# A macaron decoder layer in split float32 on one core: gate and up products of 16 of 22 inner blocks by seven products of sums of blocks

## The chip, the cores and the metric

One NeuronCore of a Trainium2 chip runs the whole layer in one launch. The metric is the device time of the program in microseconds (us); lower is better. The kernel before was run three times.

## The reference

One decoder layer over 512 tokens of width 1024: a SwiGLU half-step, a mixer (retention and causal block attention on one combined projection, then an output projection), and a second SwiGLU half-step. What the change touches are the two half-steps:

```
def _swiglu(h, w_gate, w_up, w_down):
    return (jax.nn.silu(h @ w_gate) * (h @ w_up)) @ w_down
...
    x = x + 0.5 * _swiglu(_rms(x, ffn1_norm_w[l]), ffn1_w_gate[l], ffn1_w_up[l], ffn1_w_down[l])
...
    x = x + 0.5 * _swiglu(_rms(x, ffn2_norm_w[l]), ffn2_w_gate[l], ffn2_w_up[l], ffn2_w_down[l])
```

`w_gate` and `w_up` are 1024 x 2816 and `w_down` is 2816 x 1024, all float32. Each half-step normalises `x` by its root mean square over the features first.

## The kernel before

Features lie on the partitions and the 512 tokens along the free axis, so every weight chunk is a 128x128 stationary operand and the moving operand is 128x512. Every float32 operand is split into two float32r parts, H by a copy on ScalarE and L = x - H by a subtraction on VectorE; one product is then three matmuls, WH.xH + WH.xL + WL.xH (`mm3`).

`ffn` (called twice) goes over FB = 22 inner blocks of 128 features. For each it loads the 128x1024 chunks of gate and up weights, splits them (`split_w`, tiles `raw`, `wh`, `wl`, three buffers each) and issues 2 x 8 x 3 = 48 matmuls of 512 columns into two PSUM banks (`p` for gate, `s` for up). VectorE then multiplies both by the reciprocal root mean square `st.r`, ScalarE applies Silu, VectorE multiplies the two and the result is split for the down product. The down product goes over KB = 8 output blocks with 22 x 3 = 66 matmuls each and adds half of the result to the residual; `nxt` hands each finished block to the next stage. `Stream.add` squares each residual block on ScalarE and adds the squares up, on GpSimd (`nc.gpsimd.tensor_add`); `Stream.stats` makes `st.r` of them. The mixer lies between the two half-steps.

The order of instructions is not that of the code. `Plan` notes every call, then `_order` runs a list schedule over a table of costs (`_cost`, `LAT`) with the slot counts of each tile tag as limits, and issues every engine's queue in that order. `DELAYS` shifts the parts of the mixer in it. All recorded calls have one line in the profile (L181).

## Time and profile before

| | us |
|---|---|
| three runs | 1012.77, 1010.34, 1012.0 |
| median | 1012.0 |
| the profiled execution: its span, first to last instruction | 1010.4 |
| PE busy | 993.1 |
| VectorE (DVE) busy | 526.2 |
| ScalarE (ACT) busy | 413.3 |
| GpSimd (POOL) busy | 88.8 |

The profiled execution has no time of its own beside its span; the span is 1.6 us below the median of the runs. PE is busy for 98% of it. Matmuls are pipelined, so the duration of one (0.39 us for 512 columns) is longer than the step from one to the next; the step is what counts. On VectorE too an instruction may start before the duration of the one ahead of it has run out.

### The profile page before, as it was taken

The numbers are of one execution on the slowest core, as the hardware profiler recorded it, in microseconds if no ns is written. First come the engines' busy times: TensorE is split into PE (matmuls) and PEld (weight loads), VectorE is DVE, ScalarE is ACT, GpSimd is POOL, SyncE is SP. The second block draws the span as 40 slices with busy tenths as digits, with TensorE's granted clock in tenths as the row PEclk, the third lists the DMA queues.
The fourth block names the chain that finished last, engine by engine and source line by source line (L and its number), as shares of the span: only waits on it lengthen the run. The fifth ranks groups of instructions, "written<-read, shape, count | busy, mean of one in ns | idle before, by whom it ended". The sixth has DMA issues, their size and how long they took to land.

```text
span 1010.4 us, 11674 instructions
## 1 busy us (share of the span) xinstructions
PE 993.1 (98%) x4524; PEld 812.5 (80%) x4524; DVE 526.2 (52%) x768; ACT 413.3 (41%) x641; POOL 88.8 (9%) x63
## 2 busy tenths in 40 slices
PE   8999999999999999989999999999999999999998
PEld 4888888888888888878887778688888888888888
DVE  7535434534332325587879997855445445432231
ACT  6423223223222225467868876543233233221120
POOL 4000000000010100143213320400000000000000
PEclk9999999999999999999999999999999999999999
DMA  6322322332333463352233211422322322333330
GB/s 222 117 92 84 114 95 84 106 103 78 111 116 105 131 211 115 107 151 66 83 131 115 58 38 53 141 103 86 105 94 94 104 91 97 99 94 110 125 111 26
DMA packets 36407, 105.17 MB, mean 104 GB/s; under 512 B 4480, under 2 KB 6528, under 8 KB 36352
## 3 DMA queue, kind: packets, MB, share of 16 engines
q1 hardware_dynamic: 36352, 104.43, 32.1%
q8 instruction: 35, 0.57, 0.2%
q14 instruction: 20, 0.16, 0.0%
HBM read 97.60 MB, written 4.19 MB: 101 GB/s over the span
## 4 chain that ended last, share of the span: by engine, by line
PE 87%; DVE 7%; ACT 3%; issue 1%; DMA 1%; SPq 0%; DVEq 0%; ACTq 0%
PE ps_p L181 45%; PE ps_s L181 36%; DVE s L181 5%; PE ps_t L181 4%; ACT s L181 2%; PE ps_o L181 2%; DVE wl L181 1%; ACT wh L181 1%; DMA s<-in_x_t_dram 1%; SPq L181 0%; DVE c L181 0%; DVE ad L181 0%; ACT c L181 0%; DVEq L181 0%; ACT cr L181 0%
## 5 line engine op out<-in xcount | busy, mean ns | idle before, releaser
L181 PE MATMUL ps_p<-s,wh 128*128 128x512 f32 (+1 forms) x1548 | 561.8, 392 | 3.1 <-DVE s L181 1.6
L181 PE MATMUL ps_s<-s,wh 128*128 128x512 f32 (+1 forms) x1056 | 399.1, 385 | 0.0
L181 ACT ACTIVATE wh<-raw 128x1024 fp32r<-128x1024 f32 (+4 forms) x186 | 181.0, 976 | 469.7 <-PE ps_p L181 335.7
L181 PEld LDWEIGHTS ps_p<-s,wh 128*128 128x128 f32 x1548 | 289.6, 189 | 67.0 <-DVE s L181 3.4
L181 PE MATMUL ps_p<-s,wl 128*128 128x512 f32 (+1 forms) x774 | 298.3, 392 | 1.7 <-DVE wl L181 1.7
L181 DVE TENSOR_TENSOR wl<-raw,wh 128x1024 fp32r<-128x1024 f32 (+4 forms) x186 | 219.3, 1182 | 131.4 <-ACT wh L181 128.7
L181 PEld LDWEIGHTS ps_s<-s,wh 128*128 128x128 f32 x1056 | 198.6, 188 | 39.5 <-ACT wh L181 0.2
L181 PE MATMUL ps_s<-s,wl 128*128 128x512 f32 (+1 forms) x528 | 203.6, 386 | 1.5 <-DVE wl L181 1.5
L181 PEld LDWEIGHTS ps_p<-s,wl 128*128 128x128 f32 x774 | 145.7, 189 | 32.2 <-DVE wl L181 2.9
L181 ACT ACTIVATE s<-s 128x512 f32<-128x512 f32 (+2 forms) x216 | 134.1, 628 | 77.5 <-DVE s L181 66.8
L181 DVE TENSOR_TENSOR s<-ps_p,s 128x512 f32<-128x512 f32 x72 | 49.5, 688 | 190.8 <-PE ps_p L181 190.0
L181 POOL TENSOR_TENSOR s<-s 128x512 f32<-128x512 f32 x57 | 87.5, 1542 | 376.5 <-ACT s L181 290.6
L181 DVE TENSOR_TENSOR s<-s 128x512 fp32r<-128x512 f32 (+2 forms) x155 | 111.8, 723 | 15.7 <-ACT s L181 8.6
L181 PEld LDWEIGHTS ps_s<-s,wl 128*128 128x128 f32 x528 | 99.1, 188 | 22.7 <-DVE wl L181 3.2
L181 DVE TENSOR_TENSOR s<-ps_s,s 128x512 f32<-128x512 f32 x44 | 30.4, 691 | 52.5 <-PE ps_s L181 50.2
L181 PE MATMUL ps_o<-s 128*128 128x256 f32 (+3 forms) x144 | 39.7, 295 | 2.3 <-DVE s L181 2.1
L181 PE MATMUL ps_t<-wh,s 128*128 128x512 f32 x96 | 33.7, 395 | 0.0
L181 PEld LDWEIGHTS ps_o<-s 128*128 128x128 f32 x144 | 27.3, 189 | 6.8 <-ACT s L181 2.5
L181 DVE SCALAR_TENSOR_TENSOR s<-s 128x512 f32<-128x512 f32 x30 | 24.1, 807 | 11.8 <-ACT s L181 11.5
L181 DVE SCALAR_TENSOR_TENSOR s<-s,cols 128x512 fp32r<-128x512 f32 (+1 forms) x28 | 26.8, 967 | 5.8 <-ACT s L181 5.8
L181 DVE SCALAR_TENSOR_TENSOR s<-ps_p,s 128x512 f32<-128x512 f32 (+1 forms) x9 | 6.0, 662 | 31.1 <-PE ps_p L181 31.1
L181 PE MATMUL ps_s<-s 128*128 128x128 f32 (+3 forms) x64 | 19.0, 336 | 2.8 <-DVE s L181 2.8
(65 smaller groups left out, 387.3 us busy)
## 6 DMA issues: line engine op xcount, KB each, us to landing
raw<-in_wg_dram SPq DMA_DIRECT2D x43, 512.0 KB
raw<-in_wu_dram SPq DMA_DIRECT2D x43, 512.0 KB
raw<-in_wd_dram SPq DMA_DIRECT2D x32, 512.0 KB
raw<-in_w_int_dram SPq DMA_DIRECT2D x20, 512.0 KB
raw<-in_wd_dram SPq DMA_DIRECT2D x16, 384.0 KB
s<-in_rtab_dram SPq DMA_DIRECT2D x16, 256.0 KB
raw<-in_w_inn_dram SPq DMA_DIRECT2D x8, 512.0 KB
raw<-in_w_o_dram SPq DMA_DIRECT2D x8, 384.0 KB
```

What stands on the lines that cost most here:

```text
L181: self.ops.append([eng, cost, lambda: fn(*args, **kwargs), deps, tiles, i + self.delay + DELAYS.get(self.part, 0), self.part])
```

## The change

Of the 22 inner blocks the first EVEN = 6 stay as they were. The other 16 are taken in 8 pairs (block q with block q + 8). For a pair, the weights of each of gate and up form a 2 x 2 arrangement of parts (block one or two; first or last four of the eight 128-feature chunks), and the normalised activations form a 2 x 2 arrangement too (chunk q with chunk q + 4; first or last 256 tokens). Seven products of sums of such parts (`strassen`, the Winograd form) take the place of eight. Each product is 2 (gate, up) x 4 chunks x 3 = 24 matmuls with 256 columns, both in one PSUM bank; gate in the left half, up in the right. `weave` notes the products of a pair between those of the next.

The activations' seven blocks are made once in each half-step (`token_blocks`); since they hold the normalised `x`, the products of the 16 blocks need no multiplication by `st.r`. The residual blocks give up their slots, so `x` is loaded again from DRAM before the down product (from `x_t`, or from `later`, which the mixer's output is now stored to). All added sums, of weights, activations and products, are on VectorE, and so are the sums of squares that were on GpSimd.

Weights are loaded and split in pieces of 128x512 in place of 128x1024 (768 and 256 for `w_down`), out of one pool of 98 slots of 128x512 that also holds everything else (before: 80 such slots and nine 128x1024 tiles). All eight PSUM banks have one tag with a limit for each use. The planner's table changes: a matmul costs 13.3 ns over its columns in place of 3, a GpSimd instruction somewhat more, and two-input SBUF instructions of VectorE and GpSimd are taken to exclude one another. `DELAYS` is as it was.

```diff
+EVEN = 6
+HALF = (22 - EVEN) // 2
...
-            return max(480.0, out.nbytes() / 380.0)
+            chip = all("DRAM" not in str(a.space) for a in [out, *ins])
+            return max(650.0 if chip else 480.0, out.nbytes() / 390.0)
...
-            return max(107.0, n * 0.4167) + 3
+            return max(107.0, n * 0.4167 + 13.3)
...
-        return 45 + n * 2.31
+        return 45 + n * 2.45
...
+        shared = eng == "POOL" or eng == "DVE" and sum(
+            self._free(a) > 1 and "PSUM" not in str(a.space) for a in ins) > 1
...
+                        if ops[pick][7]:
+                            other = "POOL" if e == "DVE" else "DVE"
+                            busy[e] += max(0.0, share[other] - t)
+                            share[e] = busy[e]
...
-    NS, NRAW, NSPLIT = 80, 3, 3
+    NS = 98
...
+    SLOTS = {"raw": 12, "sum": 4, "wh": 6, "wl": 6, "keep": 4, "row": 8, "block": 32}
+    BANKS = {"p": 2, "s": 2, "t": 3, "o": 1, "a": 2, "b": 2, "c": 2}
...
+        each = 512 // shape[2]
+        raws, hs, ls = [], [], []
+        for a in range(0, shape[1], each):
+            n = min(each, shape[1] - a)
+            tiles = slot(use="raw"), slot(F32R, use="wh"), slot(F32R, use="wl")
+            raw, h, lo = (t[:, :n * shape[2]].rearrange("p (a b) -> p a b", a=n) for t in tiles)
+            for x, to in zip((raw, h, lo), (raws, hs, ls)):
+                to.append(x)
+            if pieces is None:
+                nc.sync.dma_start(raw, src[:, a:a + n])
+                nc.scalar.activation(h, raw, AF.Copy)
...
-                nc.gpsimd.tensor_add(self.ssq, self.ssq, sq)
+                nc.vector.tensor_add(self.ssq, self.ssq, sq)
...
+    def token_blocks(pairs, gates=None):
+        res = [[] for _ in range(7)]
+        gate = lambda q: setattr(nc, "after", gates and gates[min(q, len(gates) - 1)])
+        for q, (one, two) in enumerate(pairs):
+            gate(q)
+            if q % 2 == 0:
+                bh, bl = slot(F32R, use="block"), slot(F32R, use="block")
+            o = slice(256 * (q % 2), 256 * (q % 2) + 256)
+            nc.scalar.activation(bh[:, o], one[:, :256], AF.Copy)
+            nc.vector.tensor_sub(bl[:, o], one[:, :256], f32(bh[:, o]))
+            res[0].append((bh[:, o], bl[:, o]))
+        def two_blocks(n, t):
+            h, lo = split(t, use="block")
+            for i in range(2):
+                res[n + i].append((h[:, 256 * i:256 * i + 256], lo[:, 256 * i:256 * i + 256]))
+        for q, (one, two) in enumerate(pairs):
+            gate(q)
+            two_blocks(1, two)
+        later = []
+        for q, (one, two) in enumerate(pairs):
+            gate(q)
+            t = slot(use="block")
+            nc.vector.tensor_sub(t[:, :256], one[:, 256:], one[:, :256])
+            nc.vector.tensor_sub(t[:, 256:], two[:, 256:], t[:, :256])
+            two_blocks(3, t)
+            u = slot(use="block")
+            nc.vector.tensor_sub(u[:, :256], two[:, 256:], one[:, 256:])
+            nc.vector.tensor_sub(u[:, 256:], two[:, :256], t[:, 256:])
+            later.append(u)
+        for q, u in enumerate(later):
+            gate(q)
+            two_blocks(5, u)
+        nc.after = None
+        return res
+    def strassen(load, nk, moving, taken):
+        n = nk * 128
+        r = {}
+        for i, j in ((1, 1), (1, 2), (2, 1), (2, 2)):
+            r[i, j] = [slot(use="raw")[:, :n] for _ in range(2)]
+            for m in range(2):
+                load(r[i, j][m], m, i, j)
+        s1 = [slot(use="sum")[:, :n] for _ in range(2)]
+        s = [s1, s1, r[2, 1], r[1, 2]]
+        for m in range(2):
+            nc.vector.tensor_add(s1[m], r[2, 1][m], r[2, 2][m])
+        for m in range(2):
+            nc.vector.tensor_sub(s[2][m], r[1, 1][m], r[2, 1][m])
+        banks, marks = {}, []
+        def product(tag, w, block, said):
+            start = tag not in banks
+            if start:
+                banks[tag] = bank(tag)
+            p = banks[tag]
+            marks.append(len(nc.ops) + 2)
+            for m in range(2):
+                h, lo = slot(F32R, use="wh")[:, :n], slot(F32R, use="wl")[:, :n]
+                nc.scalar.activation(h, w[m], AF.Copy)
+                nc.vector.tensor_sub(lo, w[m], f32(h))
+                out = p[:, 256 * m:256 * m + 256]
+                for k in range(nk):
+                    o = slice(k * 128, k * 128 + 128)
+                    xh, xl = moving[block][k]
+                    for a, (ww, xx) in enumerate(((h, xh), (h, xl), (lo, xh))):
+                        nc.tensor.matmul(out, ww[:, o], xx, start=start and m + k + a == 0,
+                                         stop=k == nk - 1 and a == 2, skip_group_check=True)
+            taken(said, p)
+        yield marks
+        product("a", r[1, 1], 0, "P1")
+        yield marks
+        product("c", r[1, 2], 1, "P2")
+        yield marks
+        product("b", s[0], 3, "P5")
+        for m in range(2):
+            nc.vector.tensor_sub(s1[m], s1[m], r[1, 1][m])
+        product("a", s[1], 4, "U2")
+        for m in range(2):
+            nc.vector.tensor_sub(s[3][m], r[1, 2][m], s1[m])
+        yield marks
+        product("a", s[2], 5, "U3")
+        yield marks
+        product("a", r[2, 2], 6, "C21")
+        product("b", s[3], 2, "B")
+        yield marks
+    def weave(calls):
+        run, marks = None, None
+        for call in [*calls, None]:
+            nxt = call and call(marks)
+            if nxt:
+                new = next(nxt)
+            for n in range(2):
+                if run:
+                    next(run)
+                if nxt:
+                    next(nxt)
+            if run:
+                next(run)
+            if nxt:
+                marks = new
+            run = nxt
+        return marks
+    def ffn(st, x, wg, wu, wd, nxt, was, first=None, last=False):
+        hs = [None] * FB
+        for fb in range(EVEN):
...
+        pairs = []
+        for q in range(4):
+            two = []
+            for kb in (q, q + 4):
+                t = slot(use="block")
+                nc.vector.scalar_tensor_tensor(t, x[kb], st.nw[:, kb:kb + 1], st.r,
+                                               op0=OP.mult, op1=OP.mult)
+                two.append(t)
+            pairs.append(two)
+        blocks = token_blocks(pairs)
+        def hidden(one, two):
+            def load(t, m, i, j):
+                nc.sync.dma_start(t.rearrange("p (a b) -> p a b", a=4),
+                                  (wg, wu)[m][(one, two)[i - 1]][:, 4 * j - 4:4 * j])
+            rows = [[slot(use="row") for _ in range(2)] for _ in range(2)]
+            keep = {}
+            def add(i, j, p, old):
+                for m in range(2):
+                    o = slice(256 * m, 256 * m + 256)
+                    nc.vector.tensor_add(rows[i][m][:, 256 * j:256 * j + 256], p[:, o], old[:, o])
+            def taken(what, p):
+                if what in ("P1", "U2", "U3"):
+                    keep[what] = slot(use="keep")
+                    nc.scalar.activation(keep[what], p, AF.Copy)
+                elif what == "P5":
+                    keep[what] = p
+                if what == "P2":
+                    add(0, 0, p, keep["P1"])
+                elif what == "U3":
+                    add(1, 1, keep["P5"], keep["U3"])
+                    g, u = (t[:, 256:] for t in rows[1])
+                    nc.scalar.activation(g, g, AF.Silu)
+                    hs[two] = slot()
+                    nc.vector.tensor_mul(hs[two][:, 256:], g, u)
+                elif what == "C21":
+                    g = rows[1][0][:, :256]
+                    nc.scalar.activation(g, p[:, :256], AF.Silu)
+                    nc.vector.tensor_mul(hs[two][:, :256], p[:, 256:], g)
+                elif what == "B":
+                    add(0, 1, p, keep["U2"])
+                    g, u = rows[0]
+                    nc.scalar.activation(g, g, AF.Silu)
+                    hs[one] = slot()
+                    nc.vector.tensor_mul(hs[one], g, u)
+            return strassen(load, 4, blocks, taken)
+        marks = weave([lambda _, q=q: hidden(q, q + HALF) for q in range(EVEN, EVEN + HALF)])
+        nc.after = marks[-1]
         for db in range(KB):
-            # the last block of all by halves of the tokens, so that less is left after the products
+            x[db] = slot()
+            nc.sync.dma_start(x[db], was[db])
+        nc.after = None
+        order = [*range(FB - 1 - HALF), *range(FB - HALF, FB - 1), FB - 1 - HALF, FB - 1]
+        parts = {}
+        for fb in order:
...
+        nc.sync.dma_start(later[db], x[db])
```

On PE, in the first half-step. Before, the gate and up products of a block alternate, all with 512 columns (`ps_p` gate, `ps_s` up, `s` the activations):

```order
L181 MATMUL ps_p<-s,wh 128x512
L181 MATMUL ps_s<-s,wl 128x512
L181 MATMUL ps_p<-s,wh 128x512
L181 MATMUL ps_s<-s,wh 128x512
L181 MATMUL ps_p<-s,wl 128x512
L181 MATMUL ps_s<-s,wh 128x512
```

Now (weights are in `s` too, banks are `ps`):

```order
L196 MATMUL ps<-s 128x512 x67
L196 MATMUL ps<-s,cr 128x512
L196 MATMUL ps<-s 128x512 x2
L196 MATMUL ps<-s,cr 128x512
L196 MATMUL ps<-s 128x512 x219
L196 MATMUL ps<-s 128x256 x1296
L196 MATMUL ps<-s 128x512 x7
L196 MATMUL ps<-s 128x256 x48
L196 MATMUL ps<-s 128x512 x563
```

After the 288 matmuls of six blocks and four of the statistics stand 1344 of 256 columns in place of 768 of 512, with the first seven of the down product ahead of the last 48; the same row of 1296, 7 and 48 stands in the second half-step.

On VectorE, in the middle of the gate and up stage. Before, one inner block (`ps_p`, `ps_s`: products taken out of PSUM; `wl`: the low part of a weight chunk):

```order
L181 TENSOR_TENSOR s<-ps_p,s 128x512
L181 TENSOR_TENSOR wl<-raw,wh 128x1024
L181 TENSOR_TENSOR s<-ps_s,s 128x512
L181 TENSOR_TENSOR s<-s 128x512
L181 TENSOR_TENSOR wl<-raw,wh 128x1024
L181 TENSOR_TENSOR s<-s 128x512
```

Now, one pair of inner blocks (the third of eight):

```order
L196 TENSOR_TENSOR s<-ps,s 128x256 x2
L196 TENSOR_TENSOR s<-s 128x512
L196 TENSOR_TENSOR s<-s 128x256
L196 TENSOR_TENSOR s<-ps,s 128x256 x2
L196 TENSOR_TENSOR s<-s 128x512 x5
L196 TENSOR_TENSOR s<-ps,s 128x256
L196 TENSOR_TENSOR s<-s 128x512 x3
L196 TENSOR_TENSOR s<-ps,s 128x256 x2
L196 TENSOR_TENSOR s<-s 128x512 x14
```

A pair has 23 instructions of 512 columns (14 low parts of weights, 8 sums of weights, one product of gate and up) and 8 of 256; in the fifth, sixth and seventh pair the last run is 20 long, with six low parts of finished inner blocks in it.

On VectorE at the start of the program. Before (`s<-s,cols`: low parts of the weighted input; `TENSOR_SCALAR s<-ps_t`: the statistics):

```order
L181 SCALAR_TENSOR_TENSOR s<-s,cols 128x512 x3
L181 TENSOR_TENSOR wl<-raw,wh 128x1024 x3
L181 TENSOR_TENSOR s<-s 128x512
L181 TENSOR_SCALAR s<-ps_t 128x512
```

Now:

```order
L196 SCALAR_TENSOR_TENSOR s<-s,cols 128x512 x2
L196 TENSOR_TENSOR s<-s 128x512 x3
L196 SCALAR_TENSOR_TENSOR s<-s,cols 128x512 x3
L196 TENSOR_TENSOR s<-s 128x512 x12
L196 TENSOR_SCALAR s<-ps 128x512
```

The sums of squares, seven `TENSOR_TENSOR s<-s 128x512` that were on GpSimd, stand on VectorE between the low parts of the weights.

## Rows read from the trace of the kernel before

**Rows 1.** The page: the span and the busy time of the engines (us, share of the span, instructions).

```profile
span 1010.4 us, 11674 instructions
...
PE 993.1 (98%) x4524; PEld 812.5 (80%) x4524; DVE 526.2 (52%) x768; ACT 413.3 (41%) x641; POOL 88.8 (9%) x63
```

**Rows 2.** Busy time in stretches: start and end, length, then busy us and instructions of PE, PEld, DVE, ACT and POOL, the granted clock, DMA share and GB/s. 20 to 240 and 660 to 880 lie in the gate and up products, 380 to 640 is mostly mixer.

```profile
0.00:20.00 20.00, 16.91 (x53) 9.32 (x54) 13.94 (x19) 14.61 (x27) 7.89 (x10) 1.00 0.78 253
20.00:80.00 60.00, 59.07 (x259) 48.23 (x260) 33.90 (x40) 23.22 (x29) 3.06 (x2) 1.00 0.31 101
80.00:240.00 160.00, 160.00 (x707) 132.51 (x706) 72.57 (x87) 48.88 (x58) 1.05 (x2) 1.00 0.29 98
...
430.00:530.00 100.00, 96.96 (x486) 78.69 (x486) 80.86 (x167) 72.72 (x151) 28.07 (x18) 0.98 0.35 109
530.00:600.00 70.00, 65.20 (x329) 50.96 (x328) 65.00 (x139) 58.31 (x126) 23.19 (x16) 1.00 0.22 68
...
640.00:660.00 20.00, 18.38 (x77) 13.96 (x76) 14.96 (x17) 11.31 (x17) 6.52 (x5) 1.00 0.50 169
660.00:800.00 140.00, 140.00 (x619) 115.95 (x618) 67.38 (x81) 45.72 (x54) 0.00 (x0) 1.00 0.28 94
```

**Rows 3.** The chain that ended last, in order of time: start, us, engine and tile, count of back-to-back instructions. The first two are matmuls of 512 columns, the last of 256.

```profile
315.65 10.65 PE ps_p L181 x47
...
413.22 19.27 PE ps_p L181 x85
...
1003.79 3.61 PE ps_p L181 x30
```

**Rows 4.** Timeline of PE in the last block, where all matmuls have 256 columns: start, us. 66 rows lie between the last two.

```profile
995.35 0.28 PE L181 MATMUL ps_s<-s,wh 128*128 128x256 f32 x1
995.47 0.28 PE L181 MATMUL ps_p<-s,wl 128*128 128x256 f32 x1
...
1003.51 0.28 PE L181 MATMUL ps_s<-s,wl 128*128 128x256 f32 x1
```

**Rows 5.** Timeline of VectorE over one inner block of the first half-step: start, us, what; in brackets the idle time ahead of it and its releaser.

```profile
108.97 0.69 DVE L181 TENSOR_TENSOR s<-ps_p,s 128x512 f32<-128x512 f32 x1 [5.62 <-PE ps_p L181]
109.66 1.22 DVE L181 TENSOR_TENSOR wl<-raw,wh 128x1024 fp32r<-128x1024 f32 x1
111.01 0.69 DVE L181 TENSOR_TENSOR s<-ps_s,s 128x512 f32<-128x512 f32 x1
111.80 0.69 DVE L181 TENSOR_TENSOR s<-s 128x512 f32<-128x512 f32 x1
112.41 1.22 DVE L181 TENSOR_TENSOR wl<-raw,wh 128x1024 fp32r<-128x1024 f32 x1
113.55 0.69 DVE L181 TENSOR_TENSOR s<-s 128x512 fp32r<-128x512 f32 x1
119.85 0.69 DVE L181 TENSOR_TENSOR s<-ps_p,s 128x512 f32<-128x512 f32 x1 [5.62 <-PE ps_p L181]
```

**Rows 6.** Timeline of VectorE where it is dense in the mixer, and at the end of the mixer, where the inputs of the second half-step are weighted (`s<-s,cols`).

```profile
585.16 0.68 DVE L181 TENSOR_TENSOR s<-ps_p,s 128x512 f32<-128x512 f32 x1
585.76 0.67 DVE L181 TENSOR_TENSOR s<-s 128x512 fp32r<-128x512 f32 x1
...
586.57 0.41 DVE L181 CUSTOM_DVE_ANT_0 s<-ps_s,s 128x256 f32<-128x256 f32 x1
...
586.92 0.20 DVE L181 TENSOR_SCALAR c<-c 128x1 f32<-128x1 f32 x1
...
631.30 0.74 DVE L181 SCALAR_TENSOR_TENSOR s<-s,cols 128x512 fp32r<-128x512 f32 x1
631.96 0.68 DVE L181 TENSOR_TENSOR s<-ps_p,s 128x512 f32<-128x512 f32 x1
```

**Rows 7.** Timelines of VectorE and GpSimd beside one another where the squares are added: at the start of the program, and at the start of the second half-step.

```profile
15.62 4.15 DVE L181 SCALAR_TENSOR_TENSOR s<-s,cols 128x512 fp32r<-128x512 f32 x3
19.70 5.66 DVE L181 TENSOR_TENSOR wl<-raw,wh 128x1024 fp32r<-128x1024 f32 x3
...
29.38 0.69 DVE L181 SCALAR_TENSOR_TENSOR s<-s 128x512 f32<-128x512 f32 x1 [2.03 <-ACT s L181]
...
16.05 7.09 POOL L181 TENSOR_TENSOR s<-s 128x512 f32<-128x512 f32 x4 [1.50 <-ACT s L181]
...
644.81 3.49 DVE L181 SCALAR_TENSOR_TENSOR s<-s,cols 128x512 fp32r<-128x512 f32 x2
...
659.97 0.69 DVE L181 SCALAR_TENSOR_TENSOR s<-s 128x512 f32<-128x512 f32 x1 [2.03 <-ACT s L181]
...
644.58 3.17 POOL L181 TENSOR_TENSOR s<-s 128x512 f32<-128x512 f32 x2 [0.86 <-ACT s L181]
```

**Rows 8.** ScalarE: two splits of 512 columns back to back and what follows (timeline), and the group of copies of a PSUM bank (count, busy, mean ns).

```profile
33.32 1.14 ACT L181 ACTIVATE s<-s 128x512 fp32r<-128x512 f32 x2
34.39 1.07 ACT L181 ACTIVATE wh<-raw 128x1024 fp32r<-128x1024 f32 x1
...
L181 ACT ACTIVATE s<-ps_p 128x512 f32<-128x512 f32 x8 | 4.7, 590 | 0.0
```

**Rows 9.** The waits of the DMA queue's own engine: for whom, us in total, times, longest.

```profile
SPq L181 <- DVE wl L181: 757.9, 168, 17.9
```

More of the change, by code (lines that the diff above doesn't have):

```diff
@@ L93, in __init__ @@
         self.part = ""
+        self.after = None
         self.table = None
@@ L179, in _note @@
             self.table_users.append(i)
+        if self.after is not None:
+            deps.add(self.after)
         cost = self._cost(eng, method, outs[0], ins, kwargs)
+        shared = eng == "POOL" or eng == "DVE" and sum(
+            self._free(a) > 1 and "PSUM" not in str(a.space) for a in ins) > 1
         self.ops.append([eng, cost, lambda: fn(*args, **kwargs), deps, tiles,
-                         i + self.delay + DELAYS.get(self.part, 0), self.part])
+                         i + self.delay + DELAYS.get(self.part, 0), self.part, shared])
     def logs_and_exps(self):
@@ L256, in _order, with _ended @@
             t, i, *x = heapq.heappop(events)
-            if i == -2:
-                for k in self.tiles[x[0]]:
-                    free[k] += 1
-            if i < 0:
-                continue
-            done += 1
-            over[i] = True
+            now = [(i, x)]
+            while events and events[0][0] <= t:
+                _, i, *x = heapq.heappop(events)
+                now.append((i, x))
+            for i, x in now:
+                done += self._ended(i, x, t, free, over, left, events, succ, at, need, ready)
             while first < n and over[first]:
                 first += 1
-            e = ops[i][0]
-            for x in ops[i][4]:
-                left[x] -= 1
-                if not left[x]:
-                    heapq.heappush(events, (t + self.LAT_FREE, -2, x))
-            for j in succ[i]:
-                at[j] = max(at[j], t + self.LAT[e].get(ops[j][0], self.LAT_ANY[e]))
-                need[j] -= 1
-                if not need[j]:
-                    heapq.heappush(ready[ops[j][0]], (ops[j][5], j))
-                    if at[j] > t:
-                        heapq.heappush(events, (at[j], -1))
-        return order, t
+        return order, t
+    def _ended(self, i, x, t, free, over, left, events, succ, at, need, ready):
+        import heapq
+        if i == -2:
+            for k in self.tiles[x[0]]:
+                free[k] += 1
+        if i < 0:
+            return 0
+        ops = self.ops
+        over[i] = True
+        e = ops[i][0]
+        for x in ops[i][4]:
+            left[x] -= 1
+            if not left[x]:
+                heapq.heappush(events, (t + self.LAT_FREE, -2, x))
+        for j in succ[i]:
+            at[j] = max(at[j], t + self.LAT[e].get(ops[j][0], self.LAT_ANY[e]))
+            need[j] -= 1
+            if not need[j]:
+                heapq.heappush(ready[ops[j][0]], (ops[j][5], j))
+                if at[j] > t:
+                    heapq.heappush(events, (at[j], -1))
+        return 1
     def issue(self):
@@ L390, in add, with part @@
         def add(self, kb, x, delay=0):
+            self.part(kb, x)
+            self.square(x, delay)
+        def part(self, kb, x):
             w = self.nw[:, kb:kb + 1]
@@ L411, in stats @@
             self.v, self.r = v, rsqrt(v)
-    def ffn(st, x, wg, wu, wd, nxt, first=None, last=False):
-        hs = []
-        for fb in range(FB):
+    def token_blocks(pairs, gates=None):
[32 more added lines that the diff above has]
+        return res
@@ L434, in ffn @@
                 st.stats("t", first is not None)
-            g, u = slot(), slot()
+            g, u = slot(), slot(use="row")
             nc.vector.tensor_mul(g, ps[0], st.r)
@@ L441, in ffn @@
+        marks = weave([lambda _, q=q: hidden(q, q + HALF) for q in range(EVEN, EVEN + HALF)])
+        nc.after = marks[-1]
+        for db in range(KB):
+            x[db] = slot()
[4 more added lines that the diff above has]
+        for fb in order:
+            parts[fb] = split(hs[fb])
         for db in range(KB):
@@ L478, in tile_layer @@
     s2 = Stream(NW[1])
-    ffn(s1, x, wg1, wu1, wd1, lambda db, y, a, b: s2.add(db, y), load_x)
-    saved = dp.tile([KB, 128, S], F32, name="saved")
+    ffn(s1, x, wg1, wu1, wd1, lambda db, y, a, b: s2.add(db, y), x_t, load_x)
+    saved, later = (dp.tile([KB, 128, S], F32, name=n) for n in ("saved", "later"))
     for kb in range(KB):
@@ L763, in tile_layer @@
         x[db] = out_proj(db, range(EARLY, KB), x[db])
+        nc.sync.dma_start(later[db], x[db])
         s3.add(db, x[db])
     ffn(s3, x, wg2, wu2, wd2, lambda db, y, a, b: nc.sync.dma_start(out[db, :, a:b], y[:, a:b]),
-        last=True)
+        later, last=True)
     nc.issue()
```

64 lines of the change are left out of this document (29 added, 35 removed).

## The prediction

> **What bounds the kernel now.** I read the page first, then busy time by stretch, then the steps from one matmul to the next, and last the queue of VectorE. The page says that PE is busy for 98% of the span and that VectorE is far from full on average [rows 1]. The average hides two kinds of stage. In the gate and up products PE has no idle time at all at full clock: 160.00 of 160 us and 140.00 of 140 us [rows 2]. In the mixer VectorE comes close to full (65.0 of 70 us between 530 and 600) and PE loses some 8 us between 430 and 600 and 1.6 us between 640 and 660 [rows 2]. So in the half-steps only fewer or shorter PE steps count, and VectorE's work there is hidden as long as it stays under PE's.
>
> The change makes PE's steps there shorter but more numerous, so the step at both widths is the number on which all hangs. At 512 columns it is 10.65 / 47 = 0.2266 us and 19.27 / 85 = 0.2267 us [rows 3]. At 256 columns it is 3.61 / 30 = 0.1203 us [rows 3], and in the last block, where two banks alternate and every matmul has a new stationary operand, 68 steps take 1003.51 - 995.35 = 8.16 us, 0.1200 us each [rows 4]. Half the columns thus cost 53% of the time, and the operand loads stay hidden at the narrow width too, since that run holds them.
>
> **PE: the products.** Removed in each half-step: 16 blocks x 48 = 768 matmuls x 0.2266 = 174.0 us. Added: 8 pairs x 7 products x 24 = 1344 x 0.1200 = 161.3 us. The gain is 12.7 us, and 25.5 us for both half-steps; all of it is on the path, since PE is never idle there. Seven products for eight would be 12.5% of 174 us, 21.7 us; the fixed part of each narrow step, 0.1200 - 0.2266 / 2 = 0.0067 us, 1344 times, takes 9.0 us back.
>
> A rule speaks to just this fixed part. The rows give a line of 0.0134 us plus 0.000416 us a column. The Trainium skill's page TensorE: Matmul & The Clock Gate (section Back-to-back issue gap) gives a warm step of the columns over 2.4 GHz plus some 2.5 ns. By the page's figure the two widths would be 215.8 and 109.2 ns and the gain an estimated 19.0 us in a half-step; the sum would then be 978 us. The trace disagrees at both widths, with 226.6 and 120.0 ns, and the sum goes by the trace.
>
> **VectorE in the block stage.** Where VectorE is dense an independent instruction of 512 columns starts 0.60 us after the one ahead and one of 256 columns 0.35 us after [rows 6]. One that needs the result of the instruction just ahead starts 0.79 us after it (111.01 to 111.80) against 0.61 us for the next, independent one [rows 5]. Before, two inner blocks took 2 x 5.26 us (10.88 us from block to block less the 5.62 us in which VectorE waited for PE [rows 5]). Now a pair takes 23 x 0.60 + 8 x 0.35 = 16.6 us against 168 x 0.1200 = 20.2 us of PE: hidden, with 3.6 us to spare. In the fifth to seventh pair six more low parts (3.6 us) fill even that: 20.2 us against 20.2 us. Weights can be split three products ahead (six slots of each part), 3 x 24 x 0.12 = 8.6 us of work, which swallows a short lag. I take 1 us of waiting in each half-step, 2 us in all, between 0 and the 49 us of the rival below; nearest is the low end, because only three pairs of eight are full.
>
> **Entry into the block stage.** The first pair waits for the activations' blocks, which VectorE makes between the statistics and the first product. Counted from the order up to the last low part that the first product needs: 45 of 512 columns x 0.60, 8 weighted inputs x 0.66 (631.30 to 631.96 [rows 6]), 2 more x 0.60 and 20 of 256 columns x 0.35 make 40.5 us. From 29.4 us, where the reciprocal root is being finished [rows 7], that ends at 69.9 us. PE has 45 + 259 matmuls behind it at 80 us [rows 2] and needs 292 for the six blocks: 80 - 12 x 0.2266 = 77.3 us. There are 7 us to spare. In the second half-step the statistics stand behind the first of the six blocks too, and the other five take PE 5 x 10.88 = 54 us [rows 5]. Cost nothing; a lag of VectorE of 10 us there, from waits that the count leaves out, would cost 3 us in each half-step.
>
> **New waits on PSUM.** Three of the products add into one bank, and ScalarE copies it out between them. A matmul's 0.28 us [rows 4] and a copy's 0.59 us [rows 8] make some 0.9 us, and at least one other product of 24 x 0.12 = 2.9 us stands between on PE. Queued behind the waiting matmul is all of PE. Cost nothing; without that cover 3 x 16 x 0.9 = 43 us. ScalarE itself splits 512 columns in 1.07 / 2 = 0.53 us [rows 8]; 14 splits, three copies and the Silus are some 11 us of 20 us in a pair.
>
> **The squares on VectorE.** GpSimd's sums stretch VectorE while they run: three weighted inputs take 4.15 us and three chunks 5.66 us beside a GpSimd run of 7.09 us [rows 7], against 3 x 0.66 = 2.0 us [rows 6] and 3 x 1.14 = 3.4 us [rows 5] free of it; later two take 3.49 us beside 3.17 us of GpSimd [rows 7]. Removing them returns 4.4 us at the start and some 2.1 us before the second half-step, and seven sums x 0.60 = 4.2 us are put in each time. VectorE is near the path at both places, but after the mixer GpSimd's own 3.17 us end on the way to the statistics too. I take -0.5 and -1.5 us, -2 us, between -6 and +4 us. Before the mixer PE had no gap that the squares could give back.
>
> **The mixer.** It has the same products, but another planner's table and another cutting of the weights set its order. Each 128x1024 chunk split in two costs 2 x 0.60 - 1.14 = 0.06 us more on VectorE, 28 times 1.7 us, partly where VectorE is 93% busy [rows 2]. What a better order could give back is bounded by PE's idle time, some 10 us between 430 and 660 [rows 2]; I bound a worse one by the same 10 us, and take +4 us, since the little idle time leaves more to lose than to win.
>
> **DMA.** The loads keep their bytes in twice the pieces, and 16 loads and 8 stores of 256 KB come on top. The DMA engines are busy for some 0.3 of the time [rows 2] and the queue's engine spends 757.9 us waiting for buffers [rows 9]. Nothing.
>
> **Sum.** -25.5 + 2 - 2 + 4 = -21.5 us. Against the profiled span of 1010.4 us that is 988.9 us; the runs' median is 1.6 us over that span, so 990.5 us.
>
> **Rivals.** *VectorE paces part of the block stage.* If half of a pair's 512-column instructions (12) take the dependent step, the pair costs 16.6 + 12 x 0.19 = 18.9 us, still hidden, but 22.5 us in the three full pairs: 2.3 x 3 x 2 = 14 us in place of 2, 1002.5 us. For it: sums and splits follow one another through two engines. Against it: the order puts other work between a sum and its use. Chance 0.15.
>
> *VectorE paces all of it, and the change is slower.* If all of them step at 0.79 us and the narrow ones at their 0.41 us, a pair takes 21.5 us and a full one 26.2 us on VectorE: (5 x 1.3 + 3 x 6.0) x 2 = 49 us in place of 2, 1037.5 us. It decides from an average of 20.2 + 23.5 / 16 = 21.7 us a pair, where the whole gain is gone. Against it: dense stretches of VectorE run at 0.60 us [rows 6]. Chance 0.06.
>
> *The mixer's order is worse by more than its bound*: +14 us in place of +4, 1000.5 us; chance 0.05.
>
> *The narrow steps have no fixed part of their own in the long run*, so that 256 columns take half of 512: 1344 x 2 x 0.0067 = 18 us more, 972.5 us. The rows speak against it over 68 narrow steps in a row [rows 4]. Chance 0.02. The step of the skill's TensorE page named above, whose fixed part is smaller, would lead the same way.
>
> That the products stay as they were is excluded by the order: 1344 narrow matmuls stand there in each half-step.
>
> **How the numbers follow.** The forecast has 0.72: block stages paced by PE, mixer between -10 and +10 us, so 976 to 998 us. The range must reach the partly paced case: 977 to 1005 us, which leaves out the slower case, the fast step and a few of the rest. About 0.3%, 3 us, can be told from no change. Faster: the forecast, the partly paced case, the mixer's case and the fast step, 0.94, less 0.02 that lands near zero, 0.92; slower: 0.06 less 0.01 near zero, 0.05; same: 0.03.
>
> **What would show it.** In the profile after, the block stages should show PE idle for under 2 us, steps of 0.120 us, and VectorE some 80 to 95% busy. Steps over 0.125 us break the first term. Gaps on PE with low parts of weights as releaser show VectorE pacing; gaps with ScalarE's copies as releaser show the PSUM waits uncovered. PE idle of over 20 us between the end of the first half-step and the start of the second would put the error into the mixer.

## Result, and the profile after

| us | before | after |
|---|---|---|
| runs | 1010.34 to 1012.77, median 1011.98 (4) | 984.69, 985.19, 987.93, 988.14, median 986.56 |
| span of the profiled execution | 1010.4 | 982.8 |
| PE busy | 993.1 | 965.3 |
| VectorE busy | 526.2 | 694.2 |

The ratio is 0.975, with a 95% interval of 0.9733 to 0.9767: 25.4 us faster between the medians. The four runs of the changed kernel lie in two pairs some 3 us apart, at a mean granted clock of 0.997 (984.69 and 985.19) and of 0.991 to 0.993 (987.93 and 988.14). The profiled execution is the fastest of them, so the spans differ by a little more than the medians, 27.6 us.

The page of the changed kernel, the lines that answer to [rows 1]:

```profile
span 982.8 us, 15385 instructions
...
PE 965.3 (98%) x5676; PEld 851.7 (87%) x5676; DVE 694.2 (71%) x1311; ACT 513.0 (52%) x1003; POOL 53.2 (5%) x42
```

The path has not moved to another engine: PE is as full as before in a shorter span, although VectorE carries 168 us more. The stretches of the changed kernel (same columns as [rows 2]); 77 to 240 and 720 to 870 lie all but a few us in the block stages, which are the stretches of matmuls of 256 columns, from 73.4 to 237.1 and from 696.6 to 860.3:

```profile
0.00:30.00 30.00, 28.61 (x107) 19.78 (x108) 22.24 (x41) 23.02 (x42) 0.20 (x4) 1.00 0.94 324
30.00:77.00 47.00, 47.00 (x223) 39.53 (x222) 44.66 (x82) 21.58 (x42) 0.00 (x0) 1.00 0.25 86
77.00:240.00 163.00, 162.31 (x1335) 161.34 (x1334) 142.37 (x262) 96.22 (x181) 0.53 (x1) 1.00 0.36 111
...
430.00:640.00 210.00, 198.51 (x986) 162.99 (x985) 179.86 (x388) 153.44 (x337) 39.96 (x28) 0.98 0.31 98
640.00:720.00 80.00, 80.00 (x447) 70.22 (x446) 66.61 (x120) 37.77 (x68) 0.00 (x0) 1.00 0.30 102
720.00:870.00 150.00, 149.26 (x1200) 147.11 (x1199) 130.35 (x240) 91.11 (x173) 0.00 (x0) 1.00 0.38 120
```

VectorE is 87% busy in both stretches and 95% busy in the entry to the first (44.66 of 47 us), and still PE is idle for only 0.69 and 0.74 us in them. The timeline of PE shows one gap in each, towards its end, and ScalarE's timeline (last line) what releases the first:

```profile
204.72 21.52 PE L196 MATMUL ps<-s 128*128 128x256 f32 x178
226.93 18.46 PE L196 MATMUL ps<-s 128*128 128x256 f32 x114 [0.69 <-ACT s L196]
```

```profile
839.73 9.64 PE L196 MATMUL ps<-s 128*128 128x256 f32 x79
```

```profile
850.11 22.09 PE L196 MATMUL ps<-s 128*128 128x256 f32 x130 [0.74 <-ACT s L196]
```

```profile
226.28 0.60 ACT L196 ACTIVATE s<-ps 128x512 f32<-128x512 f32 x1 [1.46 <-PE ps L196]
```

The step at 256 columns is (9.64 - 0.28) / 78 = 0.1200 us, as in [rows 4], now beside a VectorE that is 87% busy. The gap is the hand-off of PSUM: ScalarE copies a sum out (0.60 us) before the next product may add into the bank. It costs PE more than its idle time, since the matmul ahead of it lasts 0.28 us where the step is 0.12: 0.69 + 0.16 = 0.85 us and 0.74 + 0.16 = 0.90 us. Only the last pair shows it, since no next pair has products to put between its own; the last experiment tests this.

The reciprocal root, the mark of [rows 7], comes out as follows on VectorE's timeline:

```profile
26.73 1.42 DVE L196 SCALAR_TENSOR_TENSOR s<-s 128x512 f32<-128x512 f32 x2 [1.43 <-ACT s L196]
```

```profile
645.07 0.69 DVE L196 SCALAR_TENSOR_TENSOR s<-s 128x512 f32<-128x512 f32 x1 [1.43 <-ACT s L196]
```

VectorE's root thus comes 2.7 us earlier at the start (29.38 to 26.73). On PE more is won there. By 30 us it has started 107 matmuls, where the kernel before had started 90:

```profile
0.00:30.00 30.00, 25.98 (x90) 16.16 (x91) 21.21 (x24) 19.78 (x34) 10.95 (x11) 1.00 0.68 222
```

The 27.6 us between the spans are best divided on PE, by counting its matmuls in order of time. Four stages are marked off by the 300th matmul (the end of the six blocks), the last down matmul of the first half-step (the 2172nd; the 1596th in the kernel before) and the point near the start of the second half-step at which as many matmuls are left as a half-step has (2160; 1584 in the kernel before):

| us | up to the 300th | first half-step's rest | mixer | from there to the end |
|---|---|---|---|---|
| before | 77.5 | 293.8 | 290.8 | 348.3 |
| after | 73.6 | 282.0 | 290.7 | 336.5 |
| won | 3.9 | 11.7 | 0.2 | 11.8 |

The two half-steps win 11.7 and 11.8 us, which is the 12.7 us of the products less one visible hand-off. The rest is won at the start, and nothing of note in the mixer.

### The profile page after: what moved, and what is told of

Same layout as the page of the kernel before. It is cut to its first block, busy times and chain, and to the rows that moved or that the text cites. A ratio compares the mean times of both kernels' runs of the same rounds, so it can differ in the third digit from the quotient of the medians.

```text
span 982.8 us, 15385 instructions
## 1 busy us (share of the span) xinstructions
PE 965.3 (98%) x5676; PEld 851.7 (87%) x5676; DVE 694.2 (71%) x1311; ACT 513.0 (52%) x1003; POOL 53.2 (5%) x42
## 4 chain that ended last, share of the span: by engine, by line
PE 90%; DVE 6%; ACT 2%; issue 1%; DMA 0%; SPq 0%; DVEq 0%; ACTq 0%
PE ps L196 90%; DVE s L196 5%; ACT s L196 2%; DMA s<-in_x_t_dram 0%; SPq L196 0%; DVE c L196 0%; DVE ad L196 0%; DVEq L196 0%; ACTq L196 0%
## 5 line engine op out<-in xcount | busy, mean ns | idle before, releaser
L196 PE MATMUL ps<-s 128*128 128x256 f32 (+3 forms) x5506 | 950.9, 333 | 10.7 <-DVE s L196 5.7
L196 PEld LDWEIGHTS ps<-s 128*128 128x128 f32 x5506 | 831.1, 191 | 116.4 <-DVE s L196 10.1
L196 DVE TENSOR_TENSOR s<-s 128x512 fp32r<-128x512 f32 (+5 forms) x820 | 498.4, 667 | 43.8 <-ACT s L196 41.3
L196 ACT ACTIVATE s<-s 128x512 fp32r<-128x512 f32 (+3 forms) x700 | 384.7, 603 | 207.2 <-DVE s L196 148.2
L196 DVE TENSOR_TENSOR s<-ps,s 128x256 f32<-128x256 f32 (+6 forms) x216 | 103.7, 504 | 46.5 <-PE ps L196 25.0
L196 DVE SCALAR_TENSOR_TENSOR s<-ps,s 128x512 f32<-128x512 f32 (+1 forms) x17 | 11.2, 660 | 163.5 <-PE ps L196 163.5
L196 ACT ACTIVATE s<-ps 128x512 f32<-128x512 f32 (+7 forms) x148 | 75.3, 519 | 89.7 <-PE ps L196 85.0
L196 ACT ACTIVATE s<-s,cols 128x512 fp32r<-128x512 f32 x24 | 17.2, 721 | 97.6 <-DVE s L196 96.3
L196 POOL TENSOR_TENSOR s<-s 128x512 f32<-128x512 f32 x36 | 51.9, 1456 | 294.5 <-DMA s<-s 207.6
L196 ACT ACTIVATE s<-s,c 128x384 f32<-128x384 f32 (+3 forms) x32 | 20.7, 647 | 9.6 <-DVE c L196 9.5
L196 PE MATMUL ps<-ct,s 128*128 128x128 f32 x100 | 16.7, 276 | 1.8 <-ACT s L196 1.8
```

What stands on the lines that cost most here:

```text
L196: self.ops.append([eng, cost, lambda: fn(*args, **kwargs), deps, tiles, i + self.delay + DELAYS.get(self.part, 0), self.part, shared])
```

## Experiments

Where a kernel is compared with the changed one, the time is its median less 986.56 us. Its profiled execution is also divided as above; the last column is the granted clock between 530 and 600 us, in the mixer.

| us | up to the 300th | first half-step's rest | mixer | to the end | clock |
|---|---|---|---|---|---|
| changed kernel | 73.6 | 282.0 | 290.7 | 336.5 | 0.98 |
| all but the products | 74.3 | 293.8 | 290.8 | 348.3 | 0.95 |
| half the pairs | 74.1 | 288.4 | 291.0 | 342.9 | 0.95 |
| six more on VectorE | 73.6 | 292.6 | 293.7 | 347.8 | 0.88 |
| fourteen more on VectorE | 74.0 | 326.7 | 293.5 | 382.4 | |
| weights' sums on GpSimd | 74.3 | 289.5 | 291.8 | 343.8 | 0.95 |
| squares on GpSimd | 77.8 | 282.1 | 295.1 | 336.5 | 0.88 |
| no weaving | 73.5 | 290.3 | 294.6 | 344.8 | 0.88 |
| last pair covered | 73.4 | 281.1 | 292.5 | 335.8 | 0.90 |

The mixer takes up to 4.0 us more where that clock is lower, whatever the edit (the 295.1 us of the squares' kernel hold 1.1 us of the squares too). Whether the clock is the cause is not shown. So a difference of a few us between two times need not come from what the edit changed in the half-steps.

### All of the change but the products of sums

```diff
-EVEN = 6
+EVEN = 22
...
-        blocks = token_blocks(pairs)
...
-        marks = weave([lambda _, q=q: hidden(q, q + HALF) for q in range(EVEN, EVEN + HALF)])
```

> All 22 inner blocks are computed as before (no products of sums); the pool of slots, the cutting of weights, the planner's table, the squares on VectorE and the second load of x stay. Theory A (the gain is the arithmetic of PE's steps, 1344 x 0.1200 against 768 x 0.2266 us, 12.7 us in a half-step): 25.5 us of the gain go and only the start's 3.9 us stay, some 1006 to 1013 us. Theory B (most of the gain came with the other parts, squares and planner): 985 to 995 us.

Measured: 1011.81 us median of ten, ratio to before 1.0001 (0.9991 to 1.001). By the medians, squares on VectorE, smaller pieces, one pool, the other planner's table and the mixer's new order are together worth nothing, +0.1 us, and the change's gain (1011.81 - 986.56 = 25.3 us) is the products'. In the half-steps, divided on PE, the products gain 11.8 us each, 23.5 us in all; the other 1.8 us are not the products' own. The profiled execution here is the fastest of the ten (1009.02 us), 3.2 us shorter than the one before, all of it ahead of the 300th matmul (77.5 to 74.3 us). Eight of the ten runs took 1011.54 us or more; where they lose this again no trace shows.

### Half the pairs

```diff
-EVEN = 6
+EVEN = 14
```

> Four pairs in place of eight (14 blocks as before). Theory A: half of the 25.5 us is lost, 986.6 + 12.7 = 999 us, between 995 and 1002 us. Theory B: no more than 3 us slower, under 990 us.

Measured: 1000.51 us, ratio 0.9886 (0.9871 to 0.9901). By the medians, four pairs gain 11.3 us and the next four 14.0 us. Four pairs save 12.7 us by the steps; less the two visible hand-offs (0.85 + 0.90 us) that is 11.0 us for the first four. The half-steps on PE say the same more sharply: 5.4 + 5.4 us for the first four, 6.3 + 6.4 us for the next.

### Only the narrow step: the kernel before with 256 columns

```diff
-                        mm3(p, wh[:, kb], wl[:, kb], *st.parts[kb], kb == 0, kb == KB - 1)
+                        if fb < 6:
+                            mm3(p, wh[:, kb], wl[:, kb], *st.parts[kb], kb == 0, kb == KB - 1)
+                            continue
+                        xh, xl = st.parts[kb]
+                        for m in range(2):
+                            o = slice(256 * m, 256 * m + 256)
+                            for n, (ww, xx) in enumerate(((wh, xh), (wh, xl), (wl, xh))):
+                                nc.tensor.matmul(p[:, o], ww[:, kb], xx[:, o],
...
```

> The kernel before, with the gate and up matmuls of inner blocks 6 to 21 issued as two matmuls of 256 columns each in place of one of 512: in each half-step 1536 narrow ones stand for 768 wide ones, the same products and the same PSUM space; nothing else changes. If a matmul has a fixed part (0.1200 us at 256 columns against 0.2266 at 512), 1536 x 0.1200 - 768 x 0.2266 = 184.3 - 174.0 = 10.3 us more per half-step, 20.6 in all: 1032.6 us. If it has none (0.1133 at 256 columns): 1012 us, no difference. Between the two the fixed part would be smaller than the timeline's step says.

Measured: 1032.08 us, ratio 1.0204 (1.0187 to 1.0221); 20.7 us more than before, where the steps say 20.6. In this kernel's timeline the narrow matmuls stand 0.12 us apart:

```profile
100.00 0.28 PE L181 MATMUL ps_s<-s,wh 128*128 128x256 f32 x1
100.12 0.28 PE L181 MATMUL ps_p<-s,wh 128*128 128x256 f32 x1
100.24 0.29 PE L181 MATMUL ps_s<-s,wh 128*128 128x256 f32 x1
```

The fixed part of a step is thus real time, not an effect of the profile. The gap of some 2.5 ns over the columns, which the Trainium skill's page TensorE: Matmul & The Clock Gate (section Back-to-back issue gap) states for an isolated matmul, would give an estimated 2 x (1536 x 0.1092 - 768 x 0.2158) = 4.0 us; the measurement of 20.7 us speaks against using it here.

### More work on VectorE: six or fourteen subtractions a pair

```diff
                 nc.vector.tensor_sub(lo, w[m], f32(h))
+                if said in ("P1", "U2", "C21"):
+                    nc.vector.tensor_sub(lo, w[m], f32(h))
```

In the second kernel the line stands there for all seven products. The repeated subtraction writes the same values.

> Six of the fourteen low parts of weights in a pair are computed twice: six more VectorE instructions of 512 columns, 3.6 us in a pair, 20.2 us against PE's 20.2 us, and 23.8 us in the pairs that also split finished blocks. Theory A (3.6 us of slack in a pair and 8.6 us of lead): the slack is used up, 988 to 1010 us, PE gaps released by VectorE in the later pairs only. Theory E (VectorE has far more slack than the sum says): 986 to 988 us. Theory F (VectorE already paces): + 3.6 x 16 = 58 us, 1040 us or more.

> All fourteen low parts of a pair are computed twice: 16.6 + 8.4 = 25.0 us of VectorE in a pair and 28.6 us in the three full ones against 20.2 us of PE. Theory A: VectorE paces, (5 x 4.8 + 3 x 8.4) x 2 = 98 us slower, 1070 to 1095 us, the step of the block stage that of VectorE at 0.60 us an instruction. Theory E: under 1040 us. Theory F: + 8.4 x 16 = 134 us, over 1115 us.

Measured: 1009.44 us (ratio 0.998, 0.997 to 0.999) and 1079.39 us (ratio 1.0671, 1.0648 to 1.0694): 22.9 and 92.8 us above the changed kernel. The prediction's count of a pair gives almost these: 16.6 us and 18 low parts of finished blocks over eight pairs (18 x 0.60 / 8 = 1.35) make 17.95 us against PE's 20.2. Six more make 21.55, 1.35 us too many in each of 16 pairs, 21.6 us; fourteen more make 26.35, 98 us. In the half-steps alone, on PE, they are 21.8 us (10.6 + 11.2) and 90.6 us (44.7 + 45.9). That is what the rival "VectorE paces all of it" describes, brought about by the added work: some 2.2 us a pair are free, and what goes beyond is paid nearly in full.

Where it is paid shows in the stretches of the kernel with six more, and in its PE timeline:

```profile
77.00:130.00 53.00, 53.00 (x444) 53.00 (x443) 51.13 (x93) 27.83 (x53) 0.00 (x0) 1.00 0.32 98
130.00:180.00 50.00, 50.00 (x419) 50.00 (x418) 49.61 (x93) 33.00 (x65) 0.00 (x0) 1.00 0.26 85
180.00:240.00 60.00, 56.48 (x460) 55.23 (x459) 60.00 (x112) 33.66 (x64) 0.00 (x0) 1.00 0.42 128
240.00:260.00 20.00, 15.02 (x59) 12.29 (x60) 10.68 (x19) 4.68 (x8) 1.05 (x2) 0.83 0.38 139
```

```profile
244.98 17.38 PE L196 MATMUL ps<-s 128*128 128x512 f32 x68 [7.47 <-DVE s L196]
```

VectorE is nearly full from 77 on (51.13 of 53 us, 49.61 of 50), but PE waits for it nowhere in the block stage: the debt falls due in one piece of 7.47 us, behind the last narrow matmul, when the down product asks for its own low parts, which VectorE then makes in a row. A share of PE of 100% in the middle of the stage says nothing there; VectorE's share does. That the count agrees so well in the kernel with six more is in part luck. It has 8 x 1.35 = 10.8 us of waiting in a half-step, and the trace shows 7.47 us; of the remaining 3 us or so some 2 are a lower clock behind the wait (last section), which the count does not hold.

### The weights' sums on GpSimd

```diff
-            nc.vector.tensor_add(s1[m], r[2, 1][m], r[2, 2][m])
+            nc.gpsimd.tensor_add(s1[m], r[2, 1][m], r[2, 2][m])
```

The other three loops of sums in `strassen` are moved in the same way.

> The eight sums of weights of a pair go to GpSimd (1.5 us each, 12 us in a pair); all else stays on VectorE. Theory A (VectorE, 16.6 us in a pair, does not pace PE's 20.2 us, and GpSimd holds VectorE up while it runs, 11.8 + up to 12 us in a pair): slower, 990 to 1040 us. Theory D (VectorE is the tight engine, and relieving it helps): 980 to 985 us.

Measured: 1003.1 us, ratio 0.9914 (0.9899 to 0.9928), 16.5 us more than the changed kernel. VectorE has eight wide instructions less in each pair and is no freer: it is busy for 721.7 us in place of 694.2. Its timeline and GpSimd's, beside one another, in the third pair:

```profile
100.94 11.61 DVE L196 TENSOR_TENSOR s<-s 128x512 fp32r<-128x512 f32 x10
```

```profile
99.29 10.30 POOL L196 TENSOR_TENSOR s<-s 128x512 f32<-128x512 f32 x6
```

```profile
100.94 9.20 DVE L196 TENSOR_TENSOR s<-s 128x512 fp32r<-128x512 f32 x6
```

and VectorE's timeline in the changed kernel at the same place:

```profile
100.28 5.50 DVE L196 TENSOR_TENSOR s<-s 128x512 fp32r<-128x512 f32 x9
```

Ten wide instructions, nine of them low parts, take 11.61 us beside GpSimd's sums, against nine wide ones in 5.50 us alone. The lengthening is all in the first six, while GpSimd runs (third line): 9.20 us, where six steps of 0.61 would make 3.7. Divided by GpSimd's six sums that is some 0.9 us for each, more than the 0.60 us that it costs on VectorE itself. PE then waits for VectorE in 14 places for 13.8 us (8 for 5.7 in the changed kernel). The Trainium skill's page SBUF — State Buffer (section SBUF: two separate sides) says that GpSimd and a VectorE instruction with two SBUF inputs hold one pair of ports in turn, each for its whole instruction; the two stretched runs agree.

### The squares on GpSimd

```diff
-                nc.vector.tensor_add(self.ssq, self.ssq, sq)
+                nc.gpsimd.tensor_add(self.ssq, self.ssq, sq)
```

> Only the sums of squares go back to GpSimd. Theory A with GpSimd stretching VectorE at the start (the start lost 3.9 us less in the changed kernel): 988 to 993 us, with the statistics of the first half-step landing at some 26.5 us in place of 24.0. Theory C (the squares were worth nothing, the start gained by the smaller weight pieces): 986 to 987.5 us, statistics still near 24 us.

Measured: 992.93 us, ratio 0.9815 (0.9799 to 0.9832); 6.4 us more than the changed kernel. The start of it, in busy time by stretch:

```profile
0.00:30.00 30.00, 26.20 (x88) 17.31 (x89) 21.45 (x31) 22.17 (x39) 9.97 (x11) 0.94 0.92 322
```

88 matmuls have started by 30 us in place of 107: 19 x 0.2266 = 4.3 us. Of these 2.4 us are idle time of PE (28.61 - 26.20) and the rest goes with the clock of 0.94. The 300th matmul is still 4.2 us late (77.8 against 73.6), about where it is in the kernel before (77.5), so in these executions the squares alone account for what the change wins at the start. At the start of the second half-step they are worth 1.1 us: from the last pair of such lines in the mixer to the second root VectorE takes 36.76 us here (617.15 to 653.91) and 35.70 us in the changed kernel (609.37 to 645.07). The two half-steps behind their starts take as long as in the changed kernel, and the mixer takes 4.5 us more, with these 1.1 in it, at a lower clock:

```profile
530.00:600.00 70.00, 63.82 (x298) 52.49 (x299) 59.24 (x132) 51.14 (x116) 18.63 (x13) 0.88 0.30 91
```

The same stretch of the changed kernel:

```profile
530.00:600.00 70.00, 62.98 (x320) 51.19 (x319) 61.19 (x132) 51.85 (x118) 15.35 (x11) 0.98 0.28 82
```

The profiled executions are 8.7 us apart, the medians 6.4 us.

### Four even blocks in place of six

```diff
-EVEN = 6
+EVEN = 4
```

> Nine pairs and four plain blocks ahead of them. By the steps of PE alone a further pair is worth 96 x 0.2266 - 168 x 0.1200 = 1.6 us in a half-step: 983.4 us (theory G). Theory A with the count of the entry: VectorE needs 40.5 - 8 = 32 us from the reciprocal root to the first product's weights, PE reaches the block stage only some 24 us after it, so PE waits some 8 us in each half-step: 990 to 1000 us, with the gap just ahead of the first 256-column matmul.

Measured: 1000.48 us, ratio 0.9883 (0.9865 to 0.9901); 13.9 us more than the changed kernel, though one more pair saves 3.2 us. PE in this kernel at the entry of both stages:

```profile
53.90 0.50 PE L196 MATMUL ps<-s 128*128 128x256 f32 x2 [0.89 <-ACT s L196]
61.22 19.02 PE L196 MATMUL ps<-s 128*128 128x256 f32 x144 [6.82 <-DVE s L196]
```

```profile
690.62 9.61 PE L196 MATMUL ps<-s 128*128 128x256 f32 x58 [3.93 <-DVE s L196]
```

The waits are 0.89 + 6.82 + 3.93 = 11.6 us; the narrow steps behind the last two lose 19.02 - 144 x 0.12 = 1.7 and 9.61 - 58 x 0.12 = 2.6 us, at a granted clock of 0.91 and 0.72. 16.0 - 3.2 = 12.8 us of the 13.9. The six even blocks are there to hide VectorE's work on the activations: with four, the block products run without a break only from 61 us on. In the profiled execution, 16.0 us longer than the changed kernel's, the mixer takes 2.4 us more.

### Without the weaving of pairs

```diff
-            for n in range(2):
-                if run:
-                    next(run)
-                if nxt:
-                    next(nxt)
...
+        for call in calls:
+            for marks in call(marks):
+                pass
```

> The products of a pair are noted one after the other and no longer between those of the next pair; the same instructions. Theory A (a bank that takes several products waits some 0.9 us for ScalarE's copy unless another product stands between): up to 3 x 16 x 0.9 = 43 us slower where the planner finds nothing to put between, 990 to 1030 us, with PE gaps released by ScalarE in every pair. Theory H (the copies are short enough not to matter): 986 to 988 us.

Measured: 1004.7 us, ratio 0.9932 (0.9916 to 0.9948); 18.1 us more than the changed kernel. The waits of PE in total, number and longest, of this kernel and then of the changed one:

```profile
PE ps L196 <- ACT s L196: 17.4, 23, 2.1
```

```profile
PE ps L196 <- ACT s L196: 6.7, 7, 2.1
```

Sixteen more waits for ScalarE make 10.7 us; fourteen of them stand in the pairs, so that now all 16 pairs have one and not only the last of each half-step. PE's timeline shows one wait in the 7 x 24 = 168 matmuls of a pair:

```profile
85.75 20.41 PE L196 MATMUL ps<-s 128*128 128x256 f32 x168 [0.69 <-ACT s L196]
106.84 20.41 PE L196 MATMUL ps<-s 128*128 128x256 f32 x168 [0.69 <-ACT s L196]
```

From one wait to the next it is 21.09 us, 0.93 us more than 168 x 0.12. So two of the three hand-offs of a pair stay covered by its own products, and the third costs the 0.9 us of the expectation. With some waits for VectorE beside them the half-steps are 8.3 and 8.2 us longer, 16.5 us in all; the rest is the mixer, 4.0 us longer at a clock of 0.88. Some two thirds of the gain hang on the cover that other products give.

### The last pair's hand-off covered too

```diff
+                nc.delay = 120 if last and said == "P5" else 0
...
+                nc.delay = 0
...
```

The planner puts off these matmuls by the delay.

> The changed kernel, with the matmuls of the product P5 of the last pair of each half-step put later, so that they stand between U2 and U3 where no next pair has matmuls to give. Theory (what is lost in the block stage is the wait for ScalarE's copy of a sum at its end, 0.69 and 0.74 us, with some tenths before each): one such wait less per half-step, 1 to 2 us less: 985 us. Rival (another wait takes its place, since TensorE gets to C21 and the down product just as early): no difference, 986.6 us.

Measured: 985.6 us (984.62 to 986.75), ratio 0.9745 (0.973 to 0.9759). In its trace the gap is gone, PE runs without a break over the place and both block stages are full:

```profile
204.82 40.37 PE L196 MATMUL ps<-s 128*128 128x256 f32 x294
```

```profile
77.00:240.00 163.00, 163.00 (x1339) 162.07 (x1338) 143.04 (x264) 98.16 (x185) 0.88 (x2) 1.00 0.37 116
...
720.00:870.00 150.00, 150.00 (x1208) 148.01 (x1207) 130.83 (x241) 91.64 (x174) 0.00 (x0) 1.00 0.38 121
```

The span is 982.8 us as before the edit and the median is 1.0 us lower, with intervals that overlap almost wholly. The half-steps are shorter by 1.0 and 0.7 us, which is the two hand-offs, and the mixer takes 1.9 us more at a clock of 0.90 in place of 0.98. That the waits go and the half-steps gain what they cost is shown; that the whole kernel gets faster is not.

## Why the prediction was right, step by step

**The products, -25.5 us.** Right in mechanism and size: 23.5 us in the half-steps between the kernel without the products and the changed one, which is the 25.5 us less the two hand-offs of the last pairs, and the step at 256 columns held for 79 matmuls in a row at 0.1200 us. The narrow kernel confirms the part that is given back.

**VectorE in the block stage, +2 us.** The pair's balance was right within 8%, as the two kernels with more work show (21.8 us in the half-steps for a count of 21.6, in part by luck, and 90.6 for 98). The 2 us of waiting did not come about: nothing waits for VectorE in the stage.

**PSUM hand-offs, nothing.** Right for seven pairs of eight; the cover that was named, another product, is missing in the last pair, which costs 0.85 and 0.90 us, the price of some 0.9 us that the prediction gave for one. Without the next pair's products the half-steps lose 16.5 us, not the 43 us worked out, since two of a pair's three hand-offs are covered by its own products.

**Entry, nothing.** Right. The changed kernel's trace shows the count: VectorE is through the 55 wide and 20 narrow instructions of the count 40.6 us after the root, at 67.35 us, and the first narrow matmul starts at 73.4, so 6 us are to spare where 7 were counted:

```profile
26.73:67.35 40.62, 40.62 (x181) 33.62 (x180) 40.55 (x76) 20.90 (x38) 0.00 (x0) 1.00 0.28 98
```

(One more wide instruction has begun within the stretch.) In the kernel with four even blocks the block products run from 61.2 us, 34.1 us after its root at 27.15, where the expectation had 32.

**Squares -2, mixer +4.** These are the mis-sized terms. The squares were given -0.5 us at the start and -1.5 us before the second half-step; the kernel with the squares on GpSimd shows 4.2 and 1.1 us, so the start was far too small: what VectorE's queue gained there reached PE. The mixer, with the second start in it, took 290.7 us against 290.8 before, so its new order costs the 1.1 us that the squares give back there, not 4, in the execution that was profiled. In the executions of other kernels it took up to 4.0 us more, at a lower clock, so the +4 is not refuted for every run. By the medians both terms together are +0.1 us against the +2 forecast; in the profiled executions they are -4.1 us. PE's idle time in the mixer, 11.5 of 210 us between 430 and 640, is near the some 10 of before [rows 2].

**The sum.** The forecast was 3.9 us too high against the median (990.5 for 986.56) and 6.1 us against the profiled span (988.9 for 982.8). The 6.1 us are 3.4 more won at the start than counted, VectorE's 2 us not spent and 2.7 less for the mixer with the second start (-0.2 for +4 - 1.5), less the 1.75 us of hand-offs that were put at nothing. That the errors partly cancel, and that the median lies nearer to the forecast than the profiled execution does, is luck.

**DMA, nothing.** Right: PE's only gaps in the block stages are the two hand-offs, and neither waits for a load.

**The rivals.** Partial pacing (1002.5) and full pacing (1037.5) did not come about: in the block stage VectorE keeps to the dense step, as in the nine wide instructions in 5.50 us (5.50 / 9 = 0.61), and not to the dependent one of 0.79. The signs named for the forecast are there: PE idle for under 2 us, steps of 0.120 us, VectorE between 80 and 95% busy (87%). The fast narrow step (972.5) is refuted by the narrow kernel, and the mixer's rival (1000.5) by the kernel without the products and by the mixer's 290.7 us.

## What to carry to other kernels

Where TensorE is the bound, a method with fewer products is worth the count of steps at its own width: read the step at both widths from the trace before anything else, since the narrower step gave back 18 of 43 us here. Then count the other engines per unit of that stage in dense steps, and add up what the stage can put off to its end, because the debt shows there and not in the stage. Compare stages on the bounding engine, not only whole times: here the mixer's time moved by up to 4 us with edits that left it alone. What hides a hand-off between engines must be there for the last unit too.

## What had not been expected of the hardware

Some waits on TensorE cost more than their length. In the kernel with six more subtractions 68 matmuls after the 7.47 us wait took 17.38 us where 68 x 0.2266 = 15.4 us are due, with a granted clock of 0.83 over those 20 us, a mean between the two levels of 1.2 and 2.4 GHz. Behind waits of 6.82 and 3.93 us in the kernel with four even blocks 1.7 and 2.6 us more were lost. Behind a wait of 1.53 us at the same place, in the kernel with the weights' sums on GpSimd, nothing was: the 568 matmuls that follow took 129.06 us, against 130.72 us behind the 7.47 us:

```profile
244.18 129.06 PE L196 MATMUL ps<-s 128*128 128x512 f32 x568 [1.53 <-DVE s L196]
...
244.98 130.72 PE L196 MATMUL ps<-s 128*128 128x512 f32 x568 [7.47 <-DVE s L196]
```

The first of these is of the kernel with the sums on GpSimd, the second of the kernel with six more subtractions. So each of these waits of 4 to 7 us cost some 2 us more than its length. The length of one wait does not decide it: in the kernel with the sums on GpSimd, behind waits of 1.07 and 0.69 us with ten matmuls between them, 26 narrow matmuls took 5.05 us at a granted clock of 0.67, where 25 x 0.12 + 0.28 = 3.3 us are due:

```profile
229.24 1.46 PE L196 MATMUL ps<-s 128*128 128x256 f32 x10 [1.07 <-DVE s L196]
231.38 5.05 PE L196 MATMUL ps<-s 128*128 128x256 f32 x26 [0.69 <-ACT s L196]
```
